# Second FFN of a two-layer trunk: TensorE's opening order, the gate's additions, cast order and block sums

## The chip, the cores and the metric

The kernel runs on one core of one Trainium2 chip. The metric is the device time of one execution in microseconds (us): the median of the runs of the same kernel. Before the change it is 1092.1 us (three runs, 1091.9 to 1093.35).

## The reference, cut to what matters

Two layers work on 512 tokens of 1024 channels. Layer 0 is attention, layer 1 Fourier mixing; each ends with the gated ConvFFN that the change is about, here for layer 1:

```python
def conv_ffn(h, w_up, conv_w, conv_b, w_down):      # h (512, 1024), w_up (1024, 5632), w_down (2816, 1024)
    u = h @ w_up
    up = jnp.pad(u, ((0, 0), (1, 1), (0, 0)))
    u = up[:, :-2] * conv_w[0] + up[:, 1:-1] * conv_w[1] + up[:, 2:] * conv_w[2] + conv_b
    gate, val = jnp.split(u, 2, axis=-1)
    return (jax.nn.silu(gate) * val) @ w_down

sh1, sc1, g1, sh2, sc2, g2 = adaln_params(c, mod_w[i], mod_b[i])
h = modulate(rms_norm(x, norm_g[i, 2]), sh2, sc2)
x = x + g2 * rms_norm(conv_ffn(h, ...), norm_g[i, 3])
```

"The gate" below is g2 of layer 1, a product of a 1024-vector with a 1024 x 1024 matrix, which is needed only at the end.

## The kernel before, in words

Data lie with channels on the 128 partitions: `hh` and `hl` hold the FFN's input h as 8 blocks (k) of 128 channels by 512 tokens. Every fp32 operand is kept as a high part, a cast to fp32r, and a low part, the rest (`split`, L144: a cast on ScalarE, then a subtraction on VectorE). `mm3` (L108 to L110) makes one product of three matmuls: high x high, high weight x low input, low weight x high input. Tokens go in two halves of 256 (`halves`).

**The order of instructions** is made by a scheduler at build time: on each engine the ready instruction that was recorded first goes first, by the scheduler's own simulation. `follow(i, j)` is an order without a semaphore on one engine, i after j. `held` keeps instructions behind a fence. Buffers come from pools by tag: `raw` (weights as loaded) has 3, `wh` and `wl` 5 each, the PSUM tag `mm` 6 banks.

**The second FFN** is `ffn(1, ...)`, from about 720 us. `fi` runs over 22 blocks of 128 hidden channels, each with i = 0 (gate half) and i = 1 (value half). A *unit* is one (fi, i): 8 x 3 matmuls for each half of the tokens, 48 in all, into one PSUM bank; then `conv` (ScalarE L1485, VectorE L1486 and L1488), and after the second unit `gated` (Silu, a multiply, a split).

- *Opening.* Units 0 to 4 are swept over k, first half of the tokens first (`sweep`, L1553 and L1554 for the first k). In the meantime the norm of h is finished: `spread` gives the factor R, `remod` rewrites h pair by pair (VectorE L388, ScalarE L390 and L392 `hh`, VectorE L393 `hl`), first for the first half, then for the second. Units 0 to 4 used h without that factor, so `conv` multiplies their sums by R (L1484), which also frees their banks. Unit 5 (`u == skew`) is the first that uses the rewritten h: `up_mm` for the first half, then for the second. Then come the units from fi = 3 (`FIRST`), whose two halves are tied by `follow`.
- *Plain units* are fi 3 to 7. From fi = 8 (`SEVEN[1]`) each fi is a *block step*: `seven_products` makes the two units of one fi out of seven products of half the depth (12 matmuls each, 84 in all, Strassen's scheme with 2 x 2 blocks). It needs sums of h's blocks (`seven_inputs`, L1373 to L1376 on VectorE and four splits, at `SUMS[1] = 7`, recorded ahead of fi 7) and sums of the weights' blocks (`seven_weights`, L1389 to L1392). Three copies on ScalarE save partial sums in between (L1422, L1424, L1426), a fourth (L1432) and two additions (L1429, L1433) finish. The weights of product 1 are a split 512 wide, the others 1024 wide.
- *Down tiles.* The hidden channels go in four groups (`GROUPS[1]`: 4, 6, 6, 6). While one group is made, the group before is multiplied with `w_down` (`down_tiles`, eight d per group); `DOWN[fi]` says how many d follow each fi. In the first group ScalarE copies the result (L1509), in later ones VectorE adds it (L1511).
- *The gate* (`gemv_pair`, a generator) is pumped at the down tiles that `GEMV` names: the first pump loads 2 x 128 rows of the matrix, four more add two blocks of rows each into `gacc` on VectorE (L627, L629) and load the next, then `gemv_end` sums over partitions on TensorE (L639), and the last pump writes the gate (`gemv_out`, L649). Seven pumps in all. Its loads (L618) and those of the weights (L154) go through SP's queue.

The layer-0 FFN is the same function with other orders; `seven_products` and `seven_weights` are used there for ten fi.

Of the kernel before, what the change touches and what calls it, by code (L numbers as in the profile page):

```python
# [2 lines left out]

# [7 lines left out]
F32 = mybir.dt.float32  # L11
# [4 lines left out]
ALU = mybir.AluOpType  # L16
# [3 lines left out]
P = 128  # L20
D = 1024
KC = D // P
T = 512
TT = T // P
HT = T // 2
# [7 lines left out]
FIRST = 3  # L33
# [3 lines left out]
SEVEN = [(5, 6, 8, 10, 12, 14, 15, 17, 18, 20), (8, 9, 10, 11, 12, 13, 14, 15, 16, 17, 18, 19, 20, 21)]  # L37


GEMV = {0: (0, 5, 7), 1: (0, 2, 4, 6)}  # L40
DOWN = {8: 4, 9: 4, 10: 1, 11: 1, 12: 1, 13: 2, 14: 1, 15: 2, 16: 1, 17: 1, 18: 1, 19: 2, 20: 1, 21: 2}
NSKEW = [6, 5]
EPS = 1e-6
# [42 lines left out]
def kernel(ctx: ExitStack, tc: tile.TileContext, a):  # L86
# [526 lines left out]
    def gemv_pair(l, v, pps, xp):  # L613
        w = [mk(xp.first, [P, D], F32, n, 4) for n in ("xh", "xl")]

        def load(kk):
            for i in range(2):
                SY.dma_start(out=w[i], in_=a["mod_r"][6 * l + v - 2, kk][:, i, :])  # L618

        load(0)  # L620
        yield
        acc = mk(cp, [P, D], F32, "gacc", 1)
        for kk in range(4):
            for i in range(2):
                k = 2 * kk + i
                if k == 0:
                    V.tensor_scalar(out=acc, in0=w[i], scalar1=scol[:, 0, k:k + 1], scalar2=None, op0=ALU.mult)  # L627
                else:
                    V.scalar_tensor_tensor(out=acc, in0=w[i], scalar=scol[:, 0, k:k + 1], in1=acc, op0=ALU.mult,  # L629
                                           op1=ALU.add)  # L630
            if kk < 3:
                load(kk + 1)
            yield
        yield from gemv_end(l, v, acc, pps)
# [735 lines left out]
    def seven_inputs(xp):  # L1370
# [10 lines left out]
            split(*b[n], src)  # L1381
        return b

    def seven_weights(l, fi):
        r = raw([P, 2, KC, P], a["w_up"][l, fi])
        s = mk(wp, [P, 4, KH, P], F32, "raw", 3)
        a4 = r.rearrange("p i (c k) n -> p (i c) k n", c=2)

        for j in (V.tensor_tensor(out=s[:, 0:2], in0=a4[:, 3::-3], in1=a4[:, 2].unsqueeze(1).to_broadcast(  # L1389
                      [P, 2, KH, P]), op=ALU.add),  # L1390
                  V.tensor_tensor(out=s[:, 2], in0=s[:, 0], in1=a4[:, 0], op=ALU.add),
                  V.tensor_tensor(out=s[:, 3], in0=s[:, 2], in1=a4[:, 1], op=ALU.add)):  # L1392
            held(j)
        w = {}
        for names, src in (("1", a4[:, 0:1]), ("57", s[:, 0:2]), ("63", s[:, 2:4]), ("24", a4[:, 1::2])):
            wh, wl = wpair([P, len(names), KH, P])
            split(wh, wl, src)
            for i, n in enumerate(names):
                w[n] = wh[:, i], wl[:, i]
        return w  # L1400


    def seven_products(l, fi, pps, bs):
# [19 lines left out]
        product("5", x, 1)  # L1423
        S.copy(out=ys[:, HT:], in_=x[:, HT:])  # L1424
        product("6", y, 1)
        S.copy(out=xs[:, HT:], in_=y[:, HT:])  # L1426
        product("2", x, 0)
        product("3", x, 1)
        V.tensor_tensor(out=x, in0=x, in1=xs, op=ALU.add)  # L1429
# [32 lines left out]
    def ffn(l, xp, ready, pre, mid, gem, plain=None):  # L1462
# [163 lines left out]
        cg = None  # L1626
        for u, (fi, i, w, ps) in enumerate(first):
            if u == skew:
                for s in halves:
                    up_mm(ps, w, s)  # L1630
            elif plain is None and u > 1:
                up_mm(ps, w, halves[1], 1)
            c = conv(fi, i, ps, (R, *(ub[:, n, i, fi:fi + 1] for n in (3, 1, 2))) if u < skew and plain else None)
# [9 lines left out]
        for gi, (f0, nch) in enumerate(GROUPS[l]):  # L1643
            end = gi == len(GROUPS[l]) - 1
            for fi in range(max(f0, FIRST), f0 + nch):
                if fi == SUMS[l]:
                    bs = seven_inputs(xp)
                if fi in SEVEN[l]:
                    cc = [conv(fi, i, u, None, i == 1) for i, u in enumerate(seven_products(l, fi, pps, bs))]
                else:  # L1650
                    cc = []
                    for i, w in enumerate(up_weights(l, wpair, [fi])):
                        ps = mk(pps, [P, T], F32, "mm", 6)
                        m = [up_mm(ps, w, s) for s in halves]
                        follow(m[1][0][0], m[0][-1][1])
                        cc.append(conv(fi, i, ps))
                gated(fi, cc[0], cc[1], f0)
                if l == 0 and fi not in SEVEN[l] and fi > FIRST + 4:
                    pump(gem, GP[0])
# [449 lines left out]
```

## Time and profile before

| what | value |
|---|---|
| median of 3 runs | 1092.1 us |
| the profiled execution's own time | 1095.22 us |
| its span, first to last instruction | 1093.5 us |
| TensorE busy | 1074.4 us (98%) |
| VectorE busy | 887.3 us (81%) |
| ScalarE busy | 601.7 us (55%) |
| loads and stores | 156.55 MB, mean 143 GB/s |

The profile is of one execution. PE is TensorE's matmuls, PEld its weight loads, DVE VectorE, ACT ScalarE, POOL GpSimd, SPq the queue on which SyncE issues DMAs. A row of the order of time reads: start, duration, engine, line, operation, output <- inputs, shape, and in brackets the idle time before it with what ended it. Rows with x2 or x3 join neighbours. A matmul's record lasts from its start to its last result, so neighbours overlap: how close together they run shows in their starts. A few matmul records are missing from a trace.

### The profile page before, as it was taken

Reading aid. Unit: us, or ns where it says so; the run is one execution under the profiler, and the core shown is the slowest. Engines: PE = TensorE matmul, PEld = TensorE weight load, DVE = VectorE, ACT = ScalarE, POOL = GpSimd, SP = SyncE. Lnnn points to the kernel's source line nnn. Section 1 sums busy time; section 2 is a strip of 40 time slices with the busy share of each in tenths; the row PEclk is TensorE's granted clock in tenths of the full one; section 3 lists DMA queues with packets and bytes.
Section 4 is the critical chain, followed back from the end, with each engine's and each line's share of the span. In section 5 each row is a group of like instructions: output and inputs, shape, how many; then the busy total and the mean of one; then the engine's idle time right before and its main releaser. Section 6 shows DMA issues by size and latency. Waiting matters only on the chain.

```text
span 1093.5 us, 22646 instructions
## 1 busy us (share of the span) xinstructions
PE 1074.4 (98%) x9432; PEld 1012.8 (93%) x9432; DVE 887.3 (81%) x1454; ACT 601.7 (55%) x1053; POOL 104.6 (10%) x114
## 2 busy tenths in 40 slices
PE   9999999999999999999999999999999999999997
PEld 5699888869999999999999999989999999999996
DVE  5778877774679976877999877878997899889855
ACT  4442365675656633552465566767755465556533
POOL 0046122522100000000000020100000000000012
PEclk9999999999999999999999999999999999999999
DMA  9776101174231473426724620743205533323342
GB/s 364 287 260 212 40 1 40 43 271 188 78 155 40 154 251 143 186 88 229 263 83 153 229 107 2 237 149 120 99 26 162 205 106 112 117 82 108 111 150 78
DMA packets 33912, 156.55 MB, mean 143 GB/s; under 512 B 3472, under 2 KB 8208, under 8 KB 22160
## 3 DMA queue, kind: packets, MB, share of 16 engines
q1 hardware_dynamic: 32656, 150.89, 38.0%
q0 software_dynamic: 1152, 4.19, 1.6%
q8 instruction: 74, 1.21, 0.4%
q14 instruction: 30, 0.25, 0.1%
HBM read 148.78 MB, written 6.29 MB: 142 GB/s over the span
## 4 chain that ended last, share of the span: by engine, by line
PE 81%; DVE 9%; DMA 4%; ACT 3%; issue 2%; SPq 0%; POOL 0%; DVEq 0%; ACTq 0%; POOLq 0%
PE mm L108 23%; PE mm L109 22%; PE mm L110 22%; DVE wl L144 2%; PE PT L1147 1%; DMA raw<-in_w_up 1%; DVE gacc L597 1%; DMA xT<-in_xT 1%; PE gm L108 1%; PE O L109 1%; PE gm L109 1%; PE gm L110 1%; PE misc L211 1%; PE O L108 1%; PE O L110 1%
## 5 line engine op out<-in xcount | busy, mean ns | idle before, releaser
L144 ACT CAST wh<-raw 128x1024 fp32r<-128x1024 f32 (+2 forms) x206 | 190.2, 931 | 153.1 <-PE mm L109 101.6
L144 DVE TENSOR_TENSOR wl<-raw,wh 128x1024 fp32r<-128x1024 f32 (+2 forms) x206 | 220.1, 1074 | 25.6 <-ACT wh L144 25.4
L108 PE MATMUL mm<-hh,wh 128*128 128x256 f32 x852 | 237.7, 280 | 2.2 <-ACT sq L1424 1.1
L109 PE MATMUL mm<-hl,wh 128*128 128x256 f32 x852 | 236.9, 278 | 0.3 <-DVE hl L393 0.3
L110 PE MATMUL mm<-hh,wl 128*128 128x256 f32 x852 | 236.4, 278 | 0.7 <-DVE wl L144 0.7
L108 PEld LDWEIGHTS mm<-hh,wh 128*128 128x128 f32 x852 | 159.7, 188 | 4.5 <-ACT sq L1424 1.5
L110 PEld LDWEIGHTS mm<-hh,wl 128*128 128x128 f32 x852 | 160.8, 189 | 1.5 <-DVE wl L144 1.4
L109 PEld LDWEIGHTS mm<-hl,wh 128*128 128x128 f32 x852 | 160.0, 188 | 0.7 <-DVE hl L393 0.5
L108 PE MATMUL mm<-xh,wh 128*128 128x256 f32 x492 | 136.8, 279 | 0.0
L109 PE MATMUL mm<-xl,wh 128*128 128x256 f32 x492 | 136.5, 278 | 0.0
L110 PE MATMUL mm<-xh,wl 128*128 128x256 f32 x492 | 136.1, 277 | 0.0
L108 PE MATMUL mm<-zh,wh 128*128 128x256 f32 x384 | 106.8, 278 | 0.1
L109 PE MATMUL mm<-zl,wh 128*128 128x256 f32 x384 | 106.3, 277 | 0.0
L110 PE MATMUL mm<-zh,wl 128*128 128x256 f32 x384 | 106.3, 277 | 0.0
L108 PEld LDWEIGHTS mm<-xh,wh 128*128 128x128 f32 x492 | 92.4, 188 | 1.3 <-issue 0.4
L109 PEld LDWEIGHTS mm<-xl,wh 128*128 128x128 f32 x492 | 92.4, 188 | 0.5 <-issue 0.4
L110 PEld LDWEIGHTS mm<-xh,wl 128*128 128x128 f32 x492 | 92.4, 188 | 0.0
L318 POOL TENSOR_TENSOR cv<-cv,sq 128x256 f32<-128x256 f32 x20 | 16.6, 830 | 711.8 <-ACT sq L316 711.1
L108 PEld LDWEIGHTS mm<-zh,wh 128*128 128x128 f32 x384 | 72.1, 188 | 0.8 <-ACT sq L1422 0.3
L110 PEld LDWEIGHTS mm<-zh,wl 128*128 128x128 f32 x384 | 72.3, 188 | 0.0
L109 PEld LDWEIGHTS mm<-zl,wh 128*128 128x128 f32 x384 | 72.1, 188 | 0.0
L1485 ACT ACTIVATE cv<-mm,cols 128x512 f32<-128x512 f32 x59 | 45.7, 776 | 13.7 <-DVE mm L1429 6.5
(469 smaller groups left out, 2784.1 us busy)
## 6 DMA issues: line engine op xcount, KB each, us to landing
raw<-in_w_up SPq DMA_DIRECT2D x42, 1024.0 KB, 4.8
xT<-in_mod_r SPq DMA_DIRECT2D x20, 1024.0 KB, 5.0
raw<-in_w_down SPq DMA_DIRECT2D x32, 384.0 KB, 3.1
raw<-in_mod_p SPq DMA_DIRECT2D x8, 1024.0 KB, 4.8
raw<-in_w_down SPq DMA_DIRECT2D x16, 512.0 KB, 4.7
raw<-in_w_in SPq DMA_DIRECT2D x6, 1024.0 KB, 8.3
yT<-in_mod_r SPq DMA_DIRECT2D x10, 512.0 KB, 5.8
raw<-in_w_out SPq DMA_DIRECT2D x4, 1024.0 KB, 5.9
```

What stands on the lines that cost most here:

```text
L108: i = PE.matmul(out, lhsT=ah, rhs=bh, start=start, stop=False, skip_group_check=skip)
L109: PE.matmul(out, lhsT=ah, rhs=bl, start=False, stop=False, skip_group_check=skip)
L110: return i, PE.matmul(out, lhsT=al, rhs=bh, start=False, stop=stop, skip_group_check=skip)
L144: i = S.copy(out=h, in_=src), eng.tensor_tensor(out=l, in0=src, in1=f(h), op=ALU.subtract)
L211: PE.matmul(ps[32 * j:32 * j + 32, :w], lhsT=ones32, rhs=sq[:, j * w:(j + 1) * w], start=first, stop=last)
L318: G.tensor_tensor(out=self.acc[:, sl], in0=self.acc[:, sl], in1=sq[:, sl], op=ALU.add)
L597: held(V.scalar_tensor_tensor(out=acc, in0=w[:, i, :], scalar=scol[:, 0, k:k + 1], in1=acc, op0=ALU.mult, op1=ALU.add))
L1147: PE.transpose(out=pt[:, j * P:(j + 1) * P], in_=Ps[j][:, off:off + P], identity=ident)
L1485: S.activation(out=cv, in_=ps, func=AF.Identity, bias=bc, scale=wc[1])
```

## The change

Four edits, all in or for `ffn(1)`, two of them in functions that layer 0 also uses:

1. *Opening.* The second half of unit 5 no longer follows its first half at once. The weights of the next unit (fi 3, i = 0) are taken ahead, its bank too, and TensorE's order is fixed: unit 5's first half, the next unit's first half, unit 5's second half. The loop then does only the second half of that unit.
2. *Gate.* `GEMV` spaces the pumps: load at down tile 0 of group 0, additions at tile 7 of group 0 and 1, 3, 5 of group 1, the sum and the end at 0 and 2 of group 2. Each addition is tied behind the VectorE instruction that was recorded last before it.
3. *Copies ahead of casts.* The cast of product 1's weights of a block step is tied behind the third copy (L1426) of the block step before it, on ScalarE.
4. *Block sums later.* In layer 1 `seven_inputs` is recorded after the matmuls and convolutions of fi 7 in place of ahead of them. In layer 0 it stays, as `SUMS[0] = 5` is itself a block step.

```diff
--- before.py
+++ after.py
@@ -1,4 +1,5 @@
 import math
+from itertools import chain
 from contextlib import ExitStack, contextmanager
 
 import numpy as np
@@ -37,7 +38,7 @@
 SEVEN = [(5, 6, 8, 10, 12, 14, 15, 17, 18, 20), (8, 9, 10, 11, 12, 13, 14, 15, 16, 17, 18, 19, 20, 21)]
 
 
-GEMV = {0: (0, 5, 7), 1: (0, 2, 4, 6)}
+GEMV = {0: (0, 7), 1: (1, 3, 5), 2: (0, 2)}
 DOWN = {8: 4, 9: 4, 10: 1, 11: 1, 12: 1, 13: 2, 14: 1, 15: 2, 16: 1, 17: 1, 18: 1, 19: 2, 20: 1, 21: 2}
 NSKEW = [6, 5]
 EPS = 1e-6
@@ -621,13 +622,16 @@
         yield
         acc = mk(cp, [P, D], F32, "gacc", 1)
         for kk in range(4):
+            last = [o for o in nc.cur_bb.bb.instructions if o.engine == mybir.EngineType.DVE][-1].name
             for i in range(2):
                 k = 2 * kk + i
                 if k == 0:
-                    V.tensor_scalar(out=acc, in0=w[i], scalar1=scol[:, 0, k:k + 1], scalar2=None, op0=ALU.mult)
+                    j = V.tensor_scalar(out=acc, in0=w[i], scalar1=scol[:, 0, k:k + 1], scalar2=None, op0=ALU.mult)
                 else:
-                    V.scalar_tensor_tensor(out=acc, in0=w[i], scalar=scol[:, 0, k:k + 1], in1=acc, op0=ALU.mult,
-                                           op1=ALU.add)
+                    j = V.scalar_tensor_tensor(out=acc, in0=w[i], scalar=scol[:, 0, k:k + 1], in1=acc, op0=ALU.mult,
+                                               op1=ALU.add)
+                tc.add_manual_dep(j.ins, last, mybir.DependencyInfo(
+                    mybir.DependencyClass.NoSync, mybir.DependencyReason.DATA), reason="order")
             if kk < 3:
                 load(kk + 1)
             yield
@@ -1381,6 +1385,8 @@
             split(*b[n], src)
         return b
 
+    copied = []
+
     def seven_weights(l, fi):
         r = raw([P, 2, KC, P], a["w_up"][l, fi])
         s = mk(wp, [P, 4, KH, P], F32, "raw", 3)
@@ -1394,7 +1400,9 @@
         w = {}
         for names, src in (("1", a4[:, 0:1]), ("57", s[:, 0:2]), ("63", s[:, 2:4]), ("24", a4[:, 1::2])):
             wh, wl = wpair([P, len(names), KH, P])
-            split(wh, wl, src)
+            c = split(wh, wl, src)[0]
+            if names == "1" and copied:
+                follow(c, copied.pop())
             for i, n in enumerate(names):
                 w[n] = wh[:, i], wl[:, i]
         return w
@@ -1423,7 +1431,7 @@
         product("5", x, 1)
         S.copy(out=ys[:, HT:], in_=x[:, HT:])
         product("6", y, 1)
-        S.copy(out=xs[:, HT:], in_=y[:, HT:])
+        copied.append(S.copy(out=xs[:, HT:], in_=y[:, HT:]))
         product("2", x, 0)
         product("3", x, 1)
         V.tensor_tensor(out=x, in0=x, in1=xs, op=ALU.add)
@@ -1626,8 +1634,13 @@
         cg = None
         for u, (fi, i, w, ps) in enumerate(first):
             if u == skew:
-                for s in halves:
-                    up_mm(ps, w, s)
+                m = [up_mm(ps, w, halves[0])]
+                ahead = up_weights(l, wpair, [FIRST])
+                wa = next(ahead)
+                pa = mk(pps, [P, T], F32, "mm", 6)
+                m += [up_mm(pa, wa, halves[0]), up_mm(ps, w, halves[1])]
+                for j in (1, 2):
+                    follow(m[j][0][0], m[j - 1][-1][1])
             elif plain is None and u > 1:
                 up_mm(ps, w, halves[1], 1)
             c = conv(fi, i, ps, (R, *(ub[:, n, i, fi:fi + 1] for n in (3, 1, 2))) if u < skew and plain else None)
@@ -1643,17 +1656,24 @@
         for gi, (f0, nch) in enumerate(GROUPS[l]):
             end = gi == len(GROUPS[l]) - 1
             for fi in range(max(f0, FIRST), f0 + nch):
-                if fi == SUMS[l]:
+                if fi == SUMS[l] and fi in SEVEN[l]:
                     bs = seven_inputs(xp)
                 if fi in SEVEN[l]:
                     cc = [conv(fi, i, u, None, i == 1) for i, u in enumerate(seven_products(l, fi, pps, bs))]
                 else:
                     cc = []
-                    for i, w in enumerate(up_weights(l, wpair, [fi])):
-                        ps = mk(pps, [P, T], F32, "mm", 6)
-                        m = [up_mm(ps, w, s) for s in halves]
-                        follow(m[1][0][0], m[0][-1][1])
+                    given = l and fi == FIRST
+                    for i, w in enumerate(chain([wa], ahead) if given else up_weights(l, wpair, [fi])):
+                        if given and i == 0:
+                            ps = pa
+                            up_mm(ps, w, halves[1])
+                        else:
+                            ps = mk(pps, [P, T], F32, "mm", 6)
+                            m = [up_mm(ps, w, s) for s in halves]
+                            follow(m[1][0][0], m[0][-1][1])
                         cc.append(conv(fi, i, ps))
+                    if fi == SUMS[l]:
+                        bs = seven_inputs(xp)
                 gated(fi, cc[0], cc[1], f0)
                 if l == 0 and fi not in SEVEN[l] and fi > FIRST + 4:
                     pump(gem, GP[0])
```

## The prediction

> **What bounds the kernel now.** I read the page first, then TensorE's waits, then its order of time from 720 us on (the second FFN), and last a table by stage of how many matmuls TensorE started.
>
> ```profile
> span 1093.5 us, 22646 instructions
> PE 1074.4 (98%) x9432; PEld 1012.8 (93%) x9432; DVE 887.3 (81%) x1454; ACT 601.7 (55%) x1053; POOL 104.6 (10%) x114
> ```
>
> TensorE is the bound; the change takes no matmul away, so it can only win where matmuls stand further apart than they must. A "busy" TensorE hides that, since each record lasts 0.28 us while starts are about 0.11 us apart. So I count starts per stage (columns: TensorE busy and its matmuls, granted clock, DMA):
>
> ```profile
> core 0: us, PE busy (x), PEclk, DMA share, GB/s
> 746.00:762.00 16.00, 16.00 (x150) 1.00 0.21 86
> 768.00:866.00 98.00, 98.00 (x835) 1.00 0.33 109
> 885.00:923.00 38.00, 38.00 (x337) 1.00 0.32 108
> 954.00:1066.00 112.00, 112.00 (x991) 1.00 0.34 118
> ```
>
> All four are full and at full clock, with matmuls of the same shape. Yet from 768 to 866 one starts every 98.00/835 = 0.1174 us, and from 954 to 1066 every 112.00/991 = 0.1130. DMA load is alike, so it isn't that. TensorE has a long and a short spacing, and keeps the one it has for a hundred microseconds. Where it changes, TensorE had just waited:
>
> ```profile
> 762.54 0.28 PE L108 MATMUL mm<-hh,wh 128*128 128x256 f32 x1
> 763.16 0.39 PE L109 MATMUL mm<-hl,wh 128*128 128x256 f32 x1 [0.34 <-DVE hl L393]
> 763.38 0.28 PE L110 MATMUL mm<-hh,wl 128*128 128x256 f32 x1
> ...
> 766.00 0.28 PE L109 MATMUL mm<-hl,wh 128*128 128x256 f32 x1
> 868.46 0.28 PE L110 MATMUL mm<-zh,wl 128*128 128x256 f32 x1
> 868.82 0.39 PE L108 MATMUL mm<-hh,wh 128*128 128x256 f32 x1
> 869.04 0.28 PE L109 MATMUL mm<-hl,wh 128*128 128x256 f32 x1
> 882.47 0.28 PE L110 MATMUL mm<-zh,wl 128*128 128x256 f32 x1
> 883.81 0.38 PE L108 MATMUL mm<-hh,wh 128*128 128x256 f32 x1 [1.06 <-ACT sq L1424]
> 884.03 0.28 PE L109 MATMUL mm<-hl,wh 128*128 128x256 f32 x1
> ```
>
> These are three groups of waits. In each I take the time over two starts and subtract 0.23 for two at short spacing: 763.38 − 762.54 − 0.23 = 0.61 us; 869.04 − 868.46 − 0.23 = 0.35; 884.03 − 882.47 − 0.23 = 1.33. The long spacing begins at the first group (from 766.00 on starts are 0.118 apart) and ends at the second. These, 2.29 us of waits and the long spacing between, are all that the second FFN offers.
>
> **The opening.** The wait at 763 is for hl, the low half of the second 256 tokens, which remod makes pair by pair on VectorE:
>
> ```profile
> 753.13 1.22 DVE L144 TENSOR_TENSOR wl<-raw,wh 128x1024 fp32r<-128x1024 f32 x1
> 760.45 0.76 DVE L1484 TENSOR_TENSOR sq<-mm,Rs 128x256 f32<-128x256 f32 x2
> 764.16 0.69 DVE L393 TENSOR_TENSOR hl<-yT,hh 128x512 fp32r<-128x512 f32 x1
> 764.76 1.22 DVE L1373 TENSOR_TENSOR yT<-yT 128x1024 f32<-128x1024 f32 x1
> 765.89 0.69 DVE L393 TENSOR_TENSOR hl<-yT,hh 128x512 fp32r<-128x512 f32 x1
> ```
>
> The start at 762.54 is the seventh matmul of unit 5's second half (fi 2, i = 1), so that half began at 761.8 and the unit's first half, 24 matmuls, at 759.1. Now 24 matmuls of the next unit's first half come between: 24 × 0.113 = 2.7 us. Their weights are the subtraction of 753.13, done at 754.3 (the first of ten of this width for fi 3 to 7), and their PSUM bank is free once unit 0 is scaled (the pair of L1484, done 761.2): 0.6 us ahead of need. The second half then starts at 764.5, needs hl pair 3 at 764.5 + 12 × 0.113 = 765.9 (there at 764.85) and pair 4 at 766.55. Pair 4 came at 766.58, but behind the first of the block sums (L1373, 1.13 us to the next start), which the change moves away. The wait goes: −0.61, bounds 0 and −0.61. The matmuls brought forward were due anyway and cost nothing. With a fixed order on TensorE in place of one interleaved matmul by matmul, small waits on single semaphores go too.
>
> **The spacing.** TensorE enters this stretch with the short spacing (746 to 762: 150 starts in 16 us, a few of them narrower) and drops out in these waits. Without a wait I expect it to keep the short one: 835 matmuls at 112.00/991 take 94.37 us in place of 98.00, that is 3.63 saved; for the whole stretch 766.0 to 868.5, 3.63 × 102.5/98.0 = 3.80 us. Bounds: 0, where the spacing is redrawn anyway, and −3.80. I take −3.80, as the nearest rows on both sides are short.
>
> [...]
>
> **The block sums.** TensorE then needs everything earlier, and VectorE must follow:
>
> ```profile
> 794.91 1.22 DVE L1374 TENSOR_TENSOR yT<-yT 128x1024 f32<-128x1024 f32 x1
> 808.78 2.35 DVE L144 TENSOR_TENSOR wl<-raw,wh 128x1024 fp32r<-128x1024 f32 x2
> 820.11 1.21 DVE L144 TENSOR_TENSOR wl<-raw,wh 128x1024 fp32r<-128x1024 f32 x1
> 823.96 0.37 ACT L1422 COPY sq<-mm 128x256 f32<-128x256 f32 x1
> 760.00:820.00 60.00, 59.66 (x506) 59.40 (x505) 59.79 (x92) 40.36 (x56) 0.00 (x0) 1.00 0.17 58
> ```
>
> The last row (TensorE, weight loads, VectorE, ScalarE, GpSimd) has VectorE busy for 59.79 of 60 us. The copy at 823.96 follows the first product of the first block step (12 matmuls), so that step began at about 822.5, and fi 7, two units of 48 matmuls before it, at 822.5 − 96 × 0.1174 = 811.2. The first unit's weights (the first of the two at 808.78) were ready at 809.9: 1.3 us of slack, where TensorE will come 0.6 + 1.7 = 2.3 us earlier. In VectorE's present order that would cost about 1 us. But three block sums (from L1374) and their four splits, 7 × 1.14 = 8 us, stand ahead of that subtraction, and now come behind it: the weights can be ready some microseconds sooner. The work isn't less: the last weights of the first block step were done at 821.3, for a product that starts about 3 × 1.4 us after 822.5, 5 us of slack; 3 to 4 us of it are used up. I cost the edit at 0, with 0 to 1.5 us of new wait as bounds.
>
> **Copies ahead of casts, and the gate's additions.** The other two waits are at the fourth product of a step, which needs the copy L1424:
>
> ```profile
> 867.87 0.62 ACT L144 CAST wh<-raw 128x512 fp32r<-128x512 f32 x1 [1.54 <-DMA raw<-in_w_up]
> 868.40 0.37 ACT L1424 COPY sq<-mm 128x256 f32<-128x256 f32 x1
> 873.06 1.28 DVE L629 SCALAR_TENSOR_TENSOR gacc<-xl,cols,gacc 128x1024 f32<-128x1024 f32 x1 [0.87 <-DMA xl<-in_mod_r]
> 876.74 1.23 DVE L144 TENSOR_TENSOR wl<-raw,wh 128x1024 fp32r<-128x1024 f32 x1
> 877.99 0.33 SPq L154 DMA_DIRECT2D raw<-in_w_up  x1
> 882.87 0.62 ACT L144 CAST wh<-raw 128x512 fp32r<-128x512 f32 x1 [1.83 <-DMA raw<-in_w_up]
> 883.39 0.37 ACT L1424 COPY sq<-mm 128x256 f32<-128x256 f32 x1
> ```
>
> The 512-wide cast is product 1's weight of the next step. It stood ahead of this step's copy and waited 1.54 and 1.83 us for its load; the copy and TensorE waited behind it. The load was late because VectorE had stood 0.87 us for the gate's own load, so the buffer came free late (876.74, issue 877.99). Both ends are mended: the cast must follow the third copy, and the gate's additions come one pair each in fi 9, 11, 13 and 14, each a block step or more behind its load. The cast now falls some 4 us into a step of 84 matmuls (9.5 us), so product 1 has its weights in time. Behind it on ScalarE stand only the wide casts of the same next step. Behind an addition on VectorE, which now waits for the down tile's work recorded ahead of it, stand the next step's subtractions; on SP the gate's next loads wait for the addition, and weight loads can stand behind them as now (L154 at 877.99). So −0.35 and −1.33, bounds 0 each. Seven pumps stay seven; the gate's sum on TensorE moves from fi 13 to 16, at no cost, as it is needed only at the end.
>
> The same tie holds in the first FFN, where most of these casts follow the copy already; I cost it at 0.
>
> What remains: a copy can still be late behind the wide casts, as here at a step's start in the first FFN, where no edit helps:
>
> ```profile
> 370.65 0.28 PE L109 MATMUL mm<-hl,wh 128*128 128x256 f32 x1
> 371.07 0.39 PE L108 MATMUL mm<-zh,wh 128*128 128x256 f32 x1
> 371.30 0.28 PE L109 MATMUL mm<-zl,wh 128*128 128x256 f32 x1
> ```
>
> That is 0.65 − 0.23 = 0.42 us; I allow one such.
>
> **Sum:** −0.61 − 3.80 − 0.35 − 1.33 + 0.42 = −5.7 us. The profiled execution took 1095.2 us (span 1093.5), 3.1 over the median of 1092.1; it would go to 1089.5, and the median to 1086.4, if the timed runs have the same long stretch.
>
> **Rivals.** *Only the waits go.* The spacing term is nil, because the timed runs, 3.1 us shorter than the profiled one, may have no long stretch (its 3.8 us would fit), or because long is drawn again for as long as before: 1092.1 − 2.3 = 1089.8. [...] For it: the 3.1 us. Against: two spacings are plain in the trace. Chance 0.25, from 1089 to 1091.5.
>
> *VectorE becomes the bound.* A gate's pair is 2 × 1.2 us. In the steps from fi 11 on
>
> ```profile
> 884.00:936.00 52.00, 52.00 (x461) 51.46 (x461) 47.34 (x62) 30.58 (x47) 0.00 (x0) 1.00 0.30 100
> ```
>
> VectorE is busy 47.34 of 52 us, without any pair; three pairs add 7.2 us over about as long a time, more than the 4.7 left. The backlog must fit into the weights' lead of some 4 us; where it, or the block sums, doesn't, TensorE waits 1 to 2.5 us in all: about 1088.5. Chance 0.10.
>
> *Slower: the long spacing stays and nothing ends it.* If one small wait at 764 to 767 is left (hl pair 4 came in before just when it is now needed), TensorE goes long as before; and the two waits that ended it at 868 and 883 are gone. It then lasts at least to the gate's sum,
>
> ```profile
> 924.81 0.64 PE L639 MATMUL misc<-gacc,ones 128*32 128x256 f32 x8
> ```
>
> which now comes two to three steps later, at about 972: 104 us more at 3.7% is 3.9 us, less 2.3 of waits: +1.6, 1093.7. If it outlasts that sum as well, to 1067, it is 198 × 3.7% = 7.3, +5.0, 1097.1. This decides as soon as the long stretch passes 868 + 2.3/0.037 = 930 us. For it: the short spacing came back only after waits of 0.2 us and more. Chance 0.17.
>
> **How the numbers follow.** Forecast 0.48 (its own range 1085.0 to 1088.0), only waits 0.25, VectorE 0.10, slower 0.17. A measurement here tells 0.2%, 2.2 us: faster is below 1089.9, slower above 1094.3. The forecast and VectorE's case are faster (0.58), a third of "only waits" too (0.07); of the slower case 0.12 lie beyond 1094.3. The range runs from 1084.8 (all waits gone, and a short stretch turned short as well) to 1093.4.
>
> **What would show it.** Right: no start over 0.2 us after the last between 762 and 768, the next unit's 24 matmuls ahead of unit 5's second half; about 8.85 starts per us from 768 to 866; L1424 before the 512-wide cast, no wait near 868 and 883; L1373 only after 795; no VectorE wait on the gate's loads. Wrong: a stage of the second FFN at 8.5 starts per us, above all past 885; new waits at the first block step or in fi 11 to 15.

## The result, and the profile after

The changed kernel takes 1101.25 us (median of 7 runs, 1099.51 to 1104.86) against 1093.57 us (1091.9 to 1097.15, 7 runs) for the kernel before on the same chip: a ratio of 1.0069, 95% interval 1.0048 to 1.0091. It is slower, by 7.7 us, where 5.7 us less were forecast. The profiled execution is its fastest, 1099.51 us, against 1095.2 us for before's, so the traces have to account for 4.2 us of span.

The busy times show nothing: TensorE 1074.2 us, VectorE 886.1 and ScalarE 600.0, no engine with more work than before. The table by stage, in the prediction's windows from 768 us on, TensorE alone (the columns as there):

```profile
768.00:866.00 98.00, 97.08 (x855) 1.00 0.31 103
885.00:923.00 38.00, 37.89 (x331) 1.00 0.34 119
954.00:1066.00 112.00, 111.27 (x961) 1.00 0.34 119
```

The first row is the forecast come true: 855 starts where before had 835, although TensorE also stood still for 0.92 us. The other two are what was not forecast: 331 and 961 starts where before had 337 and 991. The first product copy of block step 8 came at 822.4 us (before 824.0), of step 11 at 876.2 (880.7), of step 14 at 921.7 (927.5). Then step 16 came at 958.9 (959.0) and step 21 at 1034.9 (1031.3). These copies don't always stand at the same place among the matmuls, so TensorE's lead is better read at the same matmul, counted from the first: the 7700th starts at 881.74 us (before 886.98), the 8000th at 916.43 (920.98), the 8200th at 943.58 (943.52), the 9100th at 1049.45 (1045.55). So 5.2 us were won up to step 11 or 12, and from there 9.1 us were lost. Up to 746 us the two profiles differ by 0.1 us. Before, from 910 us on:

```profile
910.00:930.00 20.00, 20.00 (x180) 1.00 0.30 105
930.00:950.00 20.00, 20.00 (x179) 1.00 0.29 98
950.00:1040.00 90.00, 90.00 (x797) 1.00 0.32 107
```

and after:

```profile
910.00:930.00 20.00, 18.60 (x164) 1.00 0.40 147
930.00:950.00 20.00, 17.32 (x150) 1.00 0.30 104
950.00:1040.00 90.00, 89.27 (x767) 1.00 0.27 95
```

Starts missing: 16, 29 and 30, at 0.1134 us each 1.8, 3.3 and 3.4 us. TensorE's waits after, from 880 us on (total, times, longest; this list has only time in which no record runs, so it misses waits that end within the 0.28 us of the record before):

```profile
PE mm L111 <- DVE wl L145: 4.3, 4, 2.2
PE mm L109 <- ACT sq L1430: 0.2, 1, 0.2
```

It waits for VectorE's subtractions, the low parts of the weights. What VectorE did at about 921 us:

```profile
919.44 0.68 DVE L1507 TENSOR_TENSOR cv<-cv,cv 128x512 f32<-128x512 f32 x1
920.04 1.28 DVE L631 SCALAR_TENSOR_TENSOR gacc<-xh,cols,gacc 128x1024 f32<-128x1024 f32 x1
921.24 0.69 DVE L145 TENSOR_TENSOR xT<-cv,xT 128x512 fp32r<-128x512 f32 x1
921.84 1.28 DVE L631 SCALAR_TENSOR_TENSOR gacc<-xl,cols,gacc 128x1024 f32<-128x1024 f32 x1
923.04 0.68 DVE L1519 TENSOR_TENSOR yT<-yT,mm 128x512 f32<-128x512 f32 x1
923.63 3.22 DVE L145 TENSOR_TENSOR wl<-raw,wh 128x1024 fp32r<-128x1024 f32 x3
```

and TensorE meanwhile:

```profile
923.23 0.28 PE L110 MATMUL mm<-xl,wh 128*128 128x256 f32 x1
924.91 0.39 PE L111 MATMUL mm<-zh,wl 128*128 128x256 f32 x1 [1.40 <-DVE wl L145]
```

The two additions of the gate (L631, 1.2 us each) are in line ahead of the first of three 1024-wide subtractions, which TensorE has needed since 923.3 us. At 941.75 us it is the same with the next pair, 2.23 us. The stretch of the late additions, up to 950 us, holds 5.1 us of the missing starts. The other 3.4 us come after the gate's last addition. The weight load on SP's queue:

```profile
958.92 0.33 SPq L155 DMA_DIRECT2D raw<-in_w_up  x1
973.34 0.33 SPq L155 DMA_DIRECT2D raw<-in_w_up  x1
```

and VectorE between the two:

```profile
964.06 1.23 DVE L1395 TENSOR_TENSOR raw<-raw 128x1024 f32<-128x1024 f32 x1 [2.60 <-DMA raw<-in_w_up]
...
967.00 1.22 DVE L145 TENSOR_TENSOR wl<-raw,wh 128x1024 fp32r<-128x1024 f32 x1
968.14 0.74 DVE L1494 SCALAR_TENSOR_TENSOR cv<-mm,cols,cv 128x511 f32<-128x511 f32 x1
...
969.40 0.74 DVE L1496 SCALAR_TENSOR_TENSOR cv<-mm,cols,cv 128x511 f32<-128x511 f32 x1
970.05 0.68 DVE L1398 TENSOR_TENSOR raw<-raw,raw 128x512 f32<-128x512 f32 x1
...
971.43 0.75 DVE L1496 SCALAR_TENSOR_TENSOR cv<-mm,ncw,cv 128x511 f32<-128x511 f32 x1
972.10 1.22 DVE L145 TENSOR_TENSOR wl<-raw,wh 128x1024 fp32r<-128x1024 f32 x1
```

The load takes 964.06 − 958.92 = 5.1 us, and VectorE stands for its end. The third weight sum (L1398) and the next subtraction now stand behind the convolutions of the step before (L1494, L1496), so the subtraction that frees the raw buffer ends at 973.3, 9.3 us after the first sum; the next load is issued in that moment. Load and VectorE together turn round in 14.4 us, where the 120 matmuls of such a step take 13.6 (120 × 0.1134 us). Before, the third sum and this subtraction stood ahead of all but one of these convolutions:

```profile
973.71 1.22 DVE L1389 TENSOR_TENSOR raw<-raw 128x1024 f32<-128x1024 f32 x1
...
976.65 0.69 DVE L1392 TENSOR_TENSOR raw<-raw,raw 128x512 f32<-128x512 f32 x1
...
980.40 1.22 DVE L144 TENSOR_TENSOR wl<-raw,wh 128x1024 fp32r<-128x1024 f32 x1
```

The subtraction ended 7.9 us after the first sum (973.71 to 981.62 us), 13.0 with a load of 5.1 us, and loads followed each other at 13.6 us (968.05, 981.65). VectorE's waits for this load, after and before, from 860 to 1060 us:

```profile
DVE raw L1395 <- DMA raw<-in_w_up: 11.3, 6, 2.9
```

```profile
DVE raw L1389 <- DMA raw<-in_w_up: 1.6, 3, 0.6
```

So an engine that is nearly full stands some 10 us more for loads that its own order makes late. Its waits for TensorE (L1429 and L1511 before, L1437 and L1519 after) fall from 16.1 to 8.0 us in the same window.

### The profile page after: what moved, and what is told of

Read it like the earlier page. It is cut to its first block, busy times and chain, and to the rows that moved or that the text cites. A ratio compares the mean times of both kernels' runs of the same rounds, so it can differ in the third digit from the quotient of the medians.

```text
span 1097.7 us, 22651 instructions
## 1 busy us (share of the span) xinstructions
PE 1074.2 (98%) x9432; PEld 1010.7 (92%) x9432; DVE 886.1 (81%) x1454; ACT 600.0 (55%) x1053; POOL 104.5 (10%) x114
## 5 line engine op out<-in xcount | busy, mean ns | idle before, releaser
L145 DVE TENSOR_TENSOR wl<-raw,wh 128x1024 fp32r<-128x1024 f32 (+2 forms) x206 | 219.3, 1075 | 29.6 <-ACT wh L145 28.9
```

What stands on the lines that cost most here:

```text
L145: i = S.copy(out=h, in_=src), eng.tensor_tensor(out=l, in0=src, in1=f(h), op=ALU.subtract)
```

## The experiments

The theory behind the first ones was: the gate edit puts VectorE in another order, and that alone costs the time. Rivals: the gate's additions cost, wherever they stand; or, for the gain that is missing once the gate is left out, the spacing of TensorE.

One table holds all profiles. "Long" is what TensorE lost by the long spacing: over all starts of three-product matmuls with 256 columns that follow each other in 115.5 to 128 ns, the part above 113.4 ns. "Waits" is the part above 114 ns of all that follow in more. "Rest" is the span less both. All in us; median, and ratio of the mean times to the kernel before on the same chip with its 95% interval. The rows were measured on several chips, on which the kernel before had medians of 1091.94 to 1093.57 us, so the ratios are what compares kernels. Long, waits and rest are those of one execution each.

| kernel | median | ratio | span | long | waits | rest |
|---|---|---|---|---|---|---|
| before | 1093.57 | | 1093.5 | 10.7 | 15.8 | 1067.0 |
| after | 1101.25 | 1.0069 (1.0048–1.0091) | 1097.7 | 7.9 | 22.6 | 1067.2 |
| e1_gate_only | 1102.53 | 1.0099 (1.0062–1.0137) | 1102.5 | 7.2 | 28.0 | 1067.3 |
| e2_no_gate | 1094.88 | 1.0018 (1.0003–1.0033) | 1094.1 | 13.0 | 13.4 | 1067.7 |
| e3_no_tie | 1096.78 | 1.0022 (0.9999–1.0045) | 1098.5 | 18.5 | 12.8 | 1067.2 |
| e4_opening_only | 1092.46 | 1.0006 (0.9991–1.0020) | 1091.9 | 10.8 | 14.4 | 1066.7 |
| e5_sums_ahead | 1096.22 | 1.0040 (1.0021–1.0060) | 1093.0 | 6.2 | 19.7 | 1067.1 |
| e6_late_half_load | 1096.03 | 1.0018 (1.0001–1.0034) | 1094.8 | 14.7 | 13.5 | 1066.6 |
| e7_no_pair4_wait | 1094.27 | 1.0006 (0.9987–1.0024) | 1093.4 | 11.9 | 13.3 | 1068.2 |
| e8_copies_only | 1095.15 | 1.0009 (0.9988–1.0031) | 1095.1 | 13.1 | 14.3 | 1067.8 |
| e9_low_part_last | 1094.71 | 1.0014 (0.9997–1.0030) | 1093.3 | 9.5 | 15.9 | 1067.8 |
| e10_untied_low_last | 1093.94 | 1.0005 (0.9984–1.0027) | 1093.8 | 13.0 | 13.8 | 1067.0 |
| e11_tie_old_places | 1094.84 | 1.0018 (1.0005–1.0031) | 1094.5 | 14.8 | 12.7 | 1067.0 |
| e12_transposes_once | 1092.48 | 1.0008 (0.9989–1.0027) | 1097.2 | 13.2 | 16.3 | 1067.8 |
| e13_transposes_many | 1098.79 | 1.0054 (1.0035–1.0073) | 1095.9 | 11.8 | 15.9 | 1068.2 |
| e14_before_transposes | 1092.92 | 1.0003 (0.9986–1.0020) | 1091.4 | 8.0 | 16.1 | 1067.2 |
| e15_order_only | 1095.73 | 1.0028 (1.0010–1.0047) | 1091.1 | 6.7 | 17.4 | 1067.0 |
| e16_sums_only | 1092.61 | 1.0007 (0.9991–1.0024) | 1090.3 | 6.6 | 17.6 | 1066.1 |

The last column is the same within 2.1 us in all 18. So the profiles differ by these two things and by next to nothing else, and on the whole they move against each other: where waits are few, the long spacing lasts.

### Which part costs: e1 to e4

e1 is the kernel before with the gate edit alone (places and ties of its additions); e2 has the other three edits; e3 all four, without the lines that tie the additions:

```diff
-                tc.add_manual_dep(j.ins, last, mybir.DependencyInfo(
-                    mybir.DependencyClass.NoSync, mybir.DependencyReason.DATA), reason="order")
```

e4 has the opening alone.

> Only the gate edit (its pumps spaced, its additions tied to VectorE's order); opening, cast order and block sums as before. Theory: this edit alone makes the loss. It pushes the next step's weight sums behind the convolutions on VectorE from fi 13 on, so the weights' loads go out some 4 us later per step and the loop load, sums, splits, next load (about 14.4 us) is longer than a step (13.6): waits of TensorE for wl and for the first copy from fi 14 to 21, 5 to 10 us slower than before, 1098 to 1104. Rival A (the other three edits make the loss, through the weights' lead that the earlier TensorE uses up): no slower than before, 1091 to 1094.

> Opening, cast order and block sums of the change; the gate as before. Theory: the 5.7 us won up to fi 14 stay to the end: 1086 to 1089, no wait over 0.5 us from fi 14 on. Rival A: the loss from fi 14 on stays, 1097 or more.

> All of the change but the tie: the gate's pumps are spaced, its additions are free to go ahead on VectorE. Theory: it is the tie that puts additions into full steps; without it VectorE's order is that of the gate as before, 1086 to 1089. Rival B (the spacing of the pumps itself, with its loads on SP's queue): still slow, 1097 or more.

> Only the opening; block sums, casts and gate as before. Theory: the wait at 763 goes (0.6 us) and TensorE keeps the short spacing from 766 until its next wait, at most 3.8 us more; the waits near 868 and 883 stay and take 1 to 2 us more, since TensorE comes earlier there: 1089 to 1092. Rival C (the long spacing comes by itself, whatever the opening does): 1093 and 8.5 starts per us from 768 to 866.

The gate edit alone has the whole loss (1102.53, four runs). Part of its 5 us of span over the changed kernel is a granted clock of 0.83 from 930 to 950 us: it fell behind a wait of 2.5 us that ended at 939 us, starts were then 0.213 us apart, and some 3.4 of its 28.0 us of waits are the clock's. In the other tables shown here it is 1.00. Three of e1's four timed runs have a mean clock of 0.996, four of the changed kernel's seven 0.997 or 0.998, those of the kernel before on e1's chip 0.998 to 1.000: long waits seem to cost clock as well, which no run here tests. Without the gate edit, or without the tie, the loss is gone, and nothing is gained. e2's list of TensorE's waits is empty between 746 and 1080 us, and its table by stage is:

```profile
768.00:866.00 98.00, 98.00 (x835) 1.00 0.34 117
885.00:921.00 36.00, 36.00 (x308) 1.00 0.33 107
926.00:951.00 25.00, 25.00 (x215) 1.00 0.27 90
954.00:1064.00 110.00, 110.00 (x973) 1.00 0.36 118
```

At 0.1174, 0.1169 and 0.1163 us a start (the shorter windows hold one or two narrower starts), the long spacing runs to 951 us; in e3 it runs to the end of the block steps. Without the tie the additions are as early on VectorE as before, so e3's spacing of the pumps changes nothing there.

### The order or the additions: e5, e6, e11, e15

e5 is the changed kernel with the weight sums and the splits moved up on VectorE (abridged, like the next one):

```diff
+        with later(-100 if l else 0):
+            js = (the three weight sums)
...
+            with later(-100 if l else 0):
                 c = split(wh, wl, src)[0]
```

The edit was meant for the second FFN alone, but VectorE's order in e5 differs from the changed kernel's from 351 us on, in the first FFN too. e6 keeps VectorE's late order by edges and halves the loads of steps 14 to 21 (one of the two weight tiles isn't loaded; the other stands for both):

```diff
+            r = raw([P, 1, KC, P], a["w_up"][l, fi][:, 0:1])
...
+        late = l and fi >= 15
+        if late:
+            follow(third sum, taps_done[-2])
...
+            if late and names in ("63", "24"):
+                follow(subtraction, taps_done[-1])
```

e11 has the tie with the old table of places. e15 is e2 with e6's edges and whole loads: the late order without the late additions.

> The changed kernel with one thing more: in the second FFN the three weight sums of a block step and the four splits behind them stand ahead of other VectorE work that is ready, so that on VectorE sums and subtractions come again before the convolutions of the step before. The gate's additions stay where the change puts them, in the late steps. Theory (VectorE's changed order holds the raw buffer too long: load 5.1 us and 9.3 us up to the subtraction that frees the buffer, 14.4 us against 13.6 us of matmuls a step): the waits on the weight subtraction (4.8 us in all) fall under 1 us and 8 to 10 us come back, to 1091 to 1094 us, the rest by which spacing TensorE has. Rival (what costs is the VectorE work of three gate pairs in the late steps, wherever it stands): 1099 us or more.

> The changed kernel with half of the w_up bytes left out in block steps 14 to 21 of the second FFN: one of the two weight tiles is loaded and stands for both, so all sums, splits and matmuls are done as before on halved data, and the output is another. The late order on VectorE (third sum and second and third 1024-wide subtraction behind the convolutions) is held by order edges from step 15 on. Theory (loop of load and VectorE): the load takes about 2.6 us, the loop 9.3 + 2.6 = 11.9 us, less than the 13.6 us of a step's matmuls; the waits on the weight subtraction end and the time is 1091 to 1094 us though the order stays. Rival (the order itself makes the operands late, whatever the load takes): 1099 us or more, waits of 4 us or more at the product of the second subtraction.

> The changed kernel with the old table of places for the gate (0, 2, 4, 6 of the second group of down tiles), its additions still tied to VectorE's order. VectorE's order is late in four block steps (11 to 14) and then the old one again, where the changed kernel keeps the late order to the end. Theory (loss by the late order, step by step, some 1.2 us each from the third on): 1093 to 1096 us, the waits on the weight subtraction under 2 us. Rival (the tie by itself costs, through the additions): as the changed kernel, 1099 us or more.

> The change without its gate edit (e2_no_gate, 1094.9 us), and VectorE's order of the changed kernel forced by order edges from block step 15 on: the third weight sum behind the first unit's convolution of the step before, the second and third 1024-wide subtraction behind the second unit's. Loads are whole and the gate's additions stand where they stood before, up to step 11. Theory (the order alone closes the loop of load and VectorE, 14.4 us against 13.6 us): waits on the weight subtraction of 3 us or more between 950 and 1050 us come back, 1098 to 1102 us. Rival (the gate's additions in the late steps cost, the order is only a by-product): 1094 to 1096 us, no such waits.

Starts of TensorE from 910 to 1040 us, one row from each table, in the order e5, e6, e15 (e11 has 1137); after has 1076 there, before 1151:

```profile
910.00:1040.00 130.00, 129.21 (x1137) 1.00 0.35 112
```

```profile
910.00:1040.00 130.00, 130.00 (x1118) 1.00 0.26 82
```

```profile
910.00:1040.00 130.00, 129.09 (x1132) 1.00 0.31 103
```

In these profiles all four have lost most of the loss, e11 as its expectation had it (1094.84 us, no wait listed). e6 is busy for the whole 130 us at the long spacing (1118 starts are 0.1163 us each), with the late order and the late additions both in place: with shorter loads they cost nothing beyond that. Its halved load lands after 3.6 to 4.2 us, not 2.6, so that its loop is about 13.2 us. The long spacing helps it, as it also gives VectorE more time a step; that its median ratio (1.0018) is e2's and its interval lies below the changed kernel's is the firmer evidence. e5 shows that the additions alone, with the sums ahead of them, cost little. But e15 contradicts the theory as I had put it. Its order is the late one and its loads follow each other at 14.7 to 14.8 and 14.2 us in the steps with one down tile, yet it misses 1098 to 1102 by 2.3 us. TensorE's waits in e15, from 746 to 1080 us:

```profile
PE mm L109 <- ACT sq L1433: 2.8, 3, 1.1
```

There is none on a subtraction, and two of the three, at 822 and 878 us, lie ahead of the order that was forced. The steps with two down tiles have 156 matmuls and last 17.7 us, and there the loop gains back what it loses in the others. The waits of TensorE between 866 and 1075 us, by the measure of the table, are 2.2 us in before and 0.5 in e2 (neither), 3.7 in e15 (order only), 3.1 in e5 (late additions only), 8.6 in after (both) and 0.8 in e6 (both, short loads). Over before, which like e15, e5 and after has the short spacing here, that is 1.5 and 0.9 apart and 6.4 together (1.7 of before's 2.2 are the two waits that the copies' edit takes away); over e2, at the long spacing up to 951 us, 3.2, 2.6 and 8.1. So in the profiles the loss is neither the order's nor the additions' alone: the additions take VectorE's lead away in steps 14 to 16, the slow loop of load and late order keeps it from coming back, and without the 5.1 us load both together cost little. These are single executions. The timed runs agree (1.0028 and 1.0040 against 1.0069), but e5's interval overlaps that of the changed kernel, so that they don't show by themselves that both together cost more than the sum of the two.

### The copies and the block sums alone: e8, e16

e8 is before with only the edge from the third copy to the next step's first cast; e16 is before with only the block sums behind the matmuls of fi 7.

> The edit of the copies alone on the kernel before: the high-part copy of the next step's first block waits for the product copy. By the sum of the prediction the wait of 1.33 us at 883 us goes and nothing else: 1091 to 1092.5 us. By the theory that waits redraw the spacing: with one wait fewer the long spacing that begins at 766 us lasts longer, up to 3.7 us more if it lasts to the end: 1092 to 1096 us, and executions differ by several us.

> The fourth edit alone on the kernel before: the four block sums are issued after the matmuls of the unit in front of the block steps. The prediction put it at 0, bounds 0 and +1.5 us. Theory: 1091.5 to 1093.5 us like the kernel before, the first product waits no more than 0.5 us for its inputs. Rival (the sums come too late for the first block step): up to 1094.5 us, with a wait of 0.5 to 1.5 us at about 810 to 824 us.

In e8 the waits at 868 and 883 us are gone, the first one too, which its expectation had left standing. And with them, in its profile, the end of the long spacing: it lasts from 766.4 to 925.4 us in one piece. One of its rows:

```profile
885.00:923.00 38.00, 38.00 (x325) 1.00 0.32 102
```

Before had 337 there. e16 is level with before in the timed runs, as the prediction's 0 for this edit had it; TensorE meets a wait of 0.56 us at 822.7 us, within the bound of 1.5.

### The spacing: e7, e9, e10, e12 to e14

e7 and e9 are meant to take away the small wait on hl at which e2 turned long. e2 there (the 0.19 us from the second start to the third have the wait of 0.07 us in them):

```profile
765.58 0.28 PE L109 MATMUL mm<-hh,wh 128*128 128x256 f32 x1
765.69 0.35 PE L110 MATMUL mm<-hl,wh 128*128 128x256 f32 x1
765.88 0.28 PE L111 MATMUL mm<-hh,wl 128*128 128x256 f32 x1
766.00 0.28 PE L109 MATMUL mm<-hh,wh 128*128 128x256 f32 x1
```

From here on starts are 0.118 apart. e9 and e10 (e3 with the same) read the low part of the last two channel tiles last:

```diff
-                m += [up_mm(pa, wa, halves[0]), up_mm(ps, w, halves[1])]
+                m += [up_mm(pa, wa, halves[0]), up_mm_low_last(ps, w, halves[1])]
```

> The change without its gate edit, as in e2_no_gate, and in the second half of unit 5 the matmul that reads the low part of hh stands last of its three for channel tiles 3 to 5, so that it is issued 0.11 to 0.23 us later and does not meet the wait of 0.07 us on the low part of tile 4 at 765.9 us, at which the spacing turned long in e2_no_gate. Theory (a spacing is kept until a wait, and drawn anew at each): TensorE stays at the short spacing from 746 us to the end of the block steps, 3.74 + 3.43 = 7.2 us less than e2_no_gate, 1087 to 1088.5 us. Rival (the long spacing comes by itself, or with the state of the other engines, and the wait was chance): 1093 to 1096 us, with a change to the long spacing somewhere else without a wait in front of it.

> The change without its gate edit, as in e2_no_gate; in the second half of unit 5 the two matmuls that read the low part of hh's last pair (channel tiles 6 and 7) stand last of all, 0.34 us or more later than in e2_no_gate and e7_no_pair4_wait, where TensorE waited 0.07 us for the low part of tile 6 and turned to the long spacing (765.9 and 765.1 us). e7 had moved tiles 3 to 5, the wrong ones. Theory (a spacing is kept until a wait and drawn anew there): no wait is left there, TensorE stays at the short spacing from 746 us to the gate's matmuls at 923 us, 1335 starts at 4.4 ns = 5.9 us less than e2_no_gate, and to the end 7.2 us less if those draw short: 1087 to 1089 us. Rival (the long spacing does not hang on that wait): 1093 to 1096 us, long from some matmul between 760 and 790 us with no wait in front of it.

> All four edits of the change but the tie of the gate's additions to VectorE's order, as in e3_no_tie, with the same two matmuls last as in e9_low_part_last. In e3_no_tie the long spacing held from 766.7 to 1072 us, 11.2 us over the short one. Theory: short from 746 us on, 1086.5 to 1089 us, and no wait of over 0.3 us from 800 us on. Rival: as e3_no_tie, 1094 to 1098 us.

e7 moved the wrong tiles, the wait stayed (0.18 us to the next start) and the spacing turned long there as in e2. In e9 and e10 the wait is gone and the spacing stays short, to the next disturbance. e9 by stage:

```profile
786.00:819.00 33.00, 33.00 (x294) 1.00 0.14 44
845.00:921.00 76.00, 76.00 (x648) 1.00 0.42 146
```

Short until 841 us, and then, in e9:

```profile
841.54 0.28 PE L111 MATMUL mm<-zh,wl 128*128 128x256 f32 x1
843.15 0.39 PE L109 MATMUL mm<-zh,wh 128*128 128x256 f32 x1 [1.33 <-ACT sq L1427]
843.37 0.28 PE L110 MATMUL mm<-zl,wh 128*128 128x256 f32 x1
```

Being early, TensorE meets a late copy here and another at 820 us, 2.8 us together, and the second of them leaves the long spacing. In e10 it had turned long at 785 us already, after another wait. The theory held for the place, and missed the time (1087 to 1089 and 1086.5 to 1089 forecast, 1094.71 and 1093.94 measured).

e12 to e14 try to set the spacing, by a pair of transposes that wait for nothing:

```diff
+        if (l, fi) in TURNS:
+            tp = mk(pps, [P, T], F32, "misc", 2)
+            last += [PE.transpose(out=tp[:, b * P:(b + 1) * P], in_=ident, identity=ident) for b in range(2)][1:]
```

> e9_low_part_last with two idle transposes (128 by 128, of the identity, to a PSUM tile that nobody reads) put on TensorE at the start of block step 10 of the second FFN, none of them waiting. In the profiles so far the gate's two transposes left the short spacing behind them 25 times of 29, whatever it was before, and without a wait a spacing lasted for over 1300 starts. Theory (the spacing is left by the last disturbance of the rhythm, and these transposes leave the short one): in the profile long from 843 us (if it is drawn there) only to about 863 us, then short to 922 us; some 490 starts x 4.4 ns = 2.2 us and another 1.05 us from 923 to 951 us gained, 0.23 us paid: 1091 to 1092.5 us. Rival (the spacing follows the data or the stage, not the last disturbance): no change of spacing at step 10, 1094 to 1096 us.

> As e12_transposes_once, with seven pairs of transposes: at the start of block steps 6, 15 and 17 of the first FFN and 8, 10, 12 and 15 of the second. Theory: each pair costs 0.23 us, 1.6 us in all, and leaves the short spacing behind it, so that of the 9.5 to 13 us of long spacing that the profiles show 4 to 8 us go, less what TensorE then waits for copies and casts (3 us at 820 and 842 us in e9_low_part_last): 1089 to 1092 us, with less scatter between executions than the 8 us of e9_low_part_last. Rival: 1095 to 1097 us, the pairs paid and nothing gained.

> The kernel before with two pairs of the same transposes, at the start of block steps 8 and 9 of the second FFN, and no other edit. In its profile the long spacing holds from 766.0 to 868.5 us, where a wait ends it. Theory: short from about 810 us on, 58 us / 0.1178 us = 490 starts x 4.4 ns = 2.2 us gained, 0.46 us paid, less the waits for copies that TensorE may then meet (1 to 3 us): 1091 to 1094 us, and the spacing short behind each pair. Rival: long to 868 us all the same, 1093 to 1094 us.

That fell. e12 stayed long over its pair at 862 us, and the gate's own transposes at 951 us, followed by short starts in all 13 profiles up to e11, this time turned a short spacing into a long one, for 1006 starts:

```profile
864.00:921.00 57.00, 57.00 (x486) 1.00 0.37 126
926.00:950.00 24.00, 24.00 (x214) 1.00 0.30 94
954.00:1064.00 110.00, 110.00 (x936) 1.00 0.34 115
```

In e14 the pair at 820 us left long, the one at 842 us short; e13 with its seven pairs is 6.9 us slower than before. The 25 of 29 that e12 was built on don't stand for all such pairs: of all pairs of transposes by that line (L649 before) in those 13 profiles 92 of 104 are followed by short starts, and of the pairs at about 574 us only 5 of 13. A disturbance of this kind can change the spacing, it doesn't set it. That it is a draw, and not a property of a program, two kernels show that run the same instructions in the same order on every engine up to 926 us: e15, with the same 0.19 us between two starts at 766 us as e2, kept the short spacing:

```profile
786.00:819.00 33.00, 33.00 (x293) 1.00 0.13 41
```

where e2 has 283 in the same window. What decides a draw stays open. None of the versions is faster than the kernel before by more than its measurement is uncertain.

## Why the prediction was wrong

**The step that failed** is the gate's additions: "So −0.35 and −1.33, bounds 0 each", with no price for what they push back. The prediction named what is queued behind an addition ("stand the next step's subtractions") and let the cost of it be nothing. Measured: 8.55 us of waits between 866 and 1075 us where before had 2.19, that is 6.4 us, in the profile. The medians lie 7.7 us over the kernel before with all four edits and 10.0 us with the gate edit alone (e1), each on its own chip, against 2.3 us without the gate edit (e2).

**The rival that came true was there and too small.** "VectorE becomes the bound" had its mechanism, its place (fi 11 and on) and its arithmetic (7.2 us of additions, 4.7 us of room), and then "TensorE waits 1 to 2.5 us in all". Two things made it larger. It took VectorE's order as given; the tie changed it, third sum and wide subtractions went behind the convolutions, and the load of the raw buffer came into VectorE's path. And it took the room as the idle time of a window, though VectorE could use it only while a load was there: it then stood 11.3 us for loads. A busy share of 91% is not 9% of room if the engine's own output releases its next input.

**The opening** (−0.61): right. In place of the group of waits at 763 us the changed kernel has one of 0.05 us at 766.7 us, where hl pair 4 "came in before just when it is now needed". e4, this edit alone, is level with before (1.0006). In its profile the spacing turned long after a wait of 0.11 us at 787.5 us and stayed so to 867 us (2.95 us), a new wait of 0.76 us came at 810.7 us, and the waits at 868 and 882 us shrank to 0.05 and 0.21 us, where e4's expectation had them grow.

**The spacing** (−3.80): right in the profile after (long 3.77 us from 746 to 866 us before, 0.04 after), wrong as a term of a forecast. "Without a wait I expect it to keep the short one" holds in kind: without a wait the long one lasted 1731 starts in e3, the short one 1006 in before. But which one it keeps is drawn at the last disturbance, and a wait of 0.07 us is enough, so the −3.80 was a property of one execution. The Trainium skill (TensorE: Matmul & The Clock Gate, "Back-to-back issue gap") gives N/2.4 + 2.5 ns as the warm gap of an isolated matmul, an estimate of 109 ns for 256 columns, and for a sustained stream of weight loads and matmuls one measured spacing a width, 81 ns at 128 columns and 131 ns at 512. It names no second spacing for one stream, so by it this term is 0. The runs show two, 113.4 and 117.8 ns, at a granted clock of 1.00, and by medians a gain near 0 all the same.

**The slower rival, "the long spacing stays and nothing ends it"**, with 1093.7 and 1097.1 us, is what e2 and e3 did (1094.88, 1096.78 us, where the kernel before had 1092.54; long to 951 us in the profile of the one, to the end but for 3 us in the other). It isn't why the changed kernel was slower: there the spacing was short from 746 to 973 us, and long for 17 us in all behind that.

**The copies** (−0.35, −1.33): right as mechanism, e8 has neither wait. They won nothing in e8's profile, since these waits are also what had ended the long spacing. **The block sums** (0, bounds 0 to 1.5): right, e16 at 1.0007; with a TensorE that comes early the first block step waits 1.09 us in the changed kernel, within the bounds. **The sum** nearly held up to step 12 of this execution: TensorE was 5.2 us ahead, by about 3.8 of spacing and 2.6 of waits gone, less 1.4 of waits met. For what comes behind that the forecast had no term. The rivals "only the waits go" and "slower" leave the sum's +0.42 out; with it they come to 1090.2, 1094.1 and 1097.5 us.

e5 and e6 are 3 us above before in the median, though their profiled executions have no loss of the changed kernel's kind. In e5 much of that is the first FFN: between 350 and 645 us its profile has 5.8 us of waits where the changed kernel has 3.2, from the order that its edit changed there as well. e6, by its ratio, is level with e2. What stays open is what holds e2 and its like at or a little above the kernel before, with the waits gone. Draws of the spacing would do that (the kernel before alone ranges from 1089.72 to 1096.6 us on e5's chip), but the timed runs have no trace to show it.

## What to carry to other kernels

An addition tied into a full engine's queue has three prices: its own time, the work that it pushes behind it, and the loads whose buffers that work frees. Before calling an engine's idle time room, draw the loop of load, first use and the operation that frees the buffer, and compare its length with the step: here 13.0 us before and 14.4 us after, against 13.6. A loop that is too long isn't the whole loss (e15): it costs most where something else has used up the lead. And a gain read off one profile (a long spacing, a wait) is worth what its mean over executions is: if small waits draw it anew, taking waits away can win nothing.

## What the runs showed of the hardware

With a granted clock of 1.00, TensorE issues 256-column matmuls of this kind at one of two steady spacings, 113.4 or 117.8 ns, 3.9% apart, and keeps one for up to 200 us. A wait can change it (one of 0.07 us to long in e2, one of 0.35 us to short in before), and a pair of transposes either way (e12, e14); the same wait can also leave it as it is (e15). In 18 profiles span = 1067.2 us (within 1.1) + the long spacing's excess (6.2 to 18.5 us) + the waits (12.7 to 28.0 us). The excess alone thus differs by 12.3 us, 1.1% of the time; how much of it makes the scatter between executions of one kernel is not shown, as each kernel has one trace.
